# Down projection of a SwiGLU block: two passes over halves of the tokens instead of halves of the outputs

## The chip, the cores and the metric

The kernel runs on one core of a Trainium2 chip. The metric is the device time of one execution in microseconds (us): 2367.51 is the median of three runs of the kernel before.

## The reference, cut to what matters

One residual block: a token mixer, then a SwiGLU feed-forward, each followed by a layer norm over `ALPHA * x + gate * f(u)`. The change touches the very end only:

```python
x = layer_norm(ALPHA * x + g1 * h, ln1_g[l], ln1_b[l])
u = layer_norm(x) * (1.0 + sc2) + sh2
h = (silu(u @ w_gate) * (u @ w_up)) @ w_down      # (1024, 2816) @ (2816, 1024)
x = layer_norm(ALPHA * x + g2 * h, ln2_g[l], ln2_b[l])
```

All is float32. There are 1024 tokens and 1024 channels; `g2` is one row of 1024 channels, computed earlier and kept in DRAM (`g_d[1]`).

## The kernel before, in words

Precise products are made of two parts: every operand is split into a rounded value ("hi") and the rest ("lo"), and `Dense.mm` (L79) issues three matmuls per product: lo times hi (L81), hi times lo (L82), hi times hi (L83), each 128x512. `Dense.load` (L67) brings a 128x1024 block into `raw`, casts it to hi on ACT (L75) and subtracts to get lo on DVE (L76); `split` (L190) does the same for a tile at hand (L191, L192).

The gate and up projections write h, transposed, to DRAM as 22 blocks `h_d[k]` of 128 hidden features by 1024 tokens (stores at L1264, in `group`). The down projection then runs in two passes over **halves of the output channels**, `nh` = 0 and 1 (L1314 on). In each pass the eight PSUM banks `pss` hold eight token tiles `tt` of 128 tokens by 512 channels. Step k loads `h_d[k]` (512 KB) and half of the weights of block k (256 KB, `load_wd`, L1284), multiplies the weights by the gate row `g2r` on POOL (L1287), splits both, and issues 24 matmuls: 8 tiles of 3. The first 20 steps (pass 0) or 16 steps (pass 1) run step by step; the last 2 or 6 are kept as a "tail" and run tile by tile, so that the tiles end one after the other.

`finish` (L1293) ends a tile of a pass: it loads half of the residual x1 (L1295), computes `ALPHA * x1 + ps` straight from PSUM into `acc` (L1297) and takes statistics (L1298). Only in pass 1, when both channel halves of a token are known, `normalise_out` (L1302) scales and stores: all 8 token tiles, both halves each, behind the last six steps.

The order of the instructions on each engine is a scheduler's: it may move an instruction ahead of others within an engine's queue, in a fixed order that is then run as it stands. Waits come from buffers: `raw`, `wh`, `wl` exist twice, `st` (narrow raw blocks) and `sg` (used for x1) twice, `cw` (narrow hi and lo) three times.

Of the kernel before, what the change touches and what calls it, by code (L numbers as in the profile page):

```python
# [9 lines left out]
F32 = mybir.dt.float32  # L10
F32R = mybir.dt.float32r
# [21 lines left out]
P = 128  # L33
# [88 lines left out]
def hybrid_block(ctx, tc, x, w_mod, w_ada, w_blk, w_i, w_ba, w_bb, w_o, w_g, w_u, w_d,  # L122
# [871 lines left out]
    with tc.tile_pool(name="big2", bufs=4, reuse_waits="tile") as big2:  # L994
# [202 lines left out]
        with tc.tile_pool(name="fp", bufs=2, reuse_waits="tile") as fp, \  # L1197
# [23 lines left out]
            def group(gi):  # L1221
# [34 lines left out]
                for j, c in ((3, c22), (1, c12), (2, c21)):  # L1256
                    if up:
                        V.tensor_tensor(sg[:, j, :], sg[:, j, :], c, op=ALU.mult)
                    else:
                        act(c, c, AF.Silu)  # L1260
                if up:
# [5 lines left out]

            for gi in range(NFT):
                group(gi)


            halves = (slice(0, TH), slice(TH, D))
            stats = fp.tile([P, TT, 2, 6], F32, name="stats", bufs=1)
            NL_ = 6
# [4 lines left out]
            acc = [bigp.tile([P, TT, TH], F32, tag="big", name=f"acc{nh}") for nh in range(2)]  # L1279

            def load_h(k, into=None):
                return dn.load(h_d[k], None, into)

            def load_wd(k, nh, into=None):  # L1284
                raw = fp.tile([P, TH], F32, tag="st", name="wdr")
                nc.sync.dma_start(out=raw, in_=w_d[k, nh])
                G.tensor_tensor(raw, raw, g2r[:, halves[nh]], op=ALU.mult)  # L1287
                c = fp.tile([P, 2, TH], F32R, tag="cw", name="wd", bufs=3) if into is None else into
                S.copy(c[:, 0, :], raw)
                V.tensor_tensor(c[:, 1, :], raw, c[:, 0, :].bitcast(F32), op=ALU.subtract)  # L1290
                return c[:, 0, :], c[:, 1, :]

            def finish(nh, tt, ps):  # L1293
                x1 = fp.tile([P, 4, TH], F32, tag="sg", name="x1f")[:, 0, :]
                nc.sync.dma_start(out=x1, in_=x1_d[tt][:, halves[nh]])  # L1295
                a_ = acc[nh][:, tt, :]
                V.scalar_tensor_tensor(a_, x1, ALPHA, ps, op0=ALU.mult, op1=ALU.add)  # L1297
                V.bn_stats(stats[:, tt, nh, :], a_)  # L1298
                if nh:
                    normalise_out(tt, norm_scalars(stats[:, tt, :, :], fp))  # L1300

            def normalise_out(tt, mv):  # L1302
                for nh in range(2):
                    a_, sl = acc[nh][:, tt, :], halves[nh]
                    if nh and tt < TT - 1:
                        S.activation(a_, a_, AF.Identity, bias=mv[:, 3:4], scale=mv[:, 2:3])
                        V.tensor_tensor(a_, a_, lg2[:, sl], op=ALU.mult)
                        G.tensor_tensor(a_, a_, lb2[:, sl], op=ALU.add)
                    else:
                        V.scalar_tensor_tensor(a_, a_, mv[:, 0:1], lg2[:, sl], op0=ALU.subtract, op1=ALU.mult)  # L1310
                        V.scalar_tensor_tensor(a_, a_, mv[:, 2:3], lb2[:, sl], op0=ALU.mult, op1=ALU.add)
                    nc.sync.dma_start(out=out[tt][:, sl], in_=a_)

            for nh in range(2):  # L1314
# [104 lines left out]
```

## Time and profile before

| | us |
|---|---|
| median of 3 runs (lowest, highest) | 2367.51 (2366.99, 2368.29) |
| the profiled execution's own time | 2364.6 |
| its span, first to last instruction | 2362.8 |
| PE busy (x12412 matmuls) | 2248.6, 95% of the span |
| DVE busy | 1599.0, 68% |
| ACT busy | 1043.6, 44% |
| POOL busy | 391.4, 17% |

The profiled execution lies 2.9 us under the median. A PE that is busy 95% of the time says little of where a stage loses time; for that the stretches and the timeline of single engines are needed. The down projection begins at about 2098.8 us of the span.

### The profile page before, as it was taken

The page shows a single profiled execution, that of the slowest core. Times are in us where ns is not written, and L with a number is a line of the kernel's source. Part 1 is how long each engine was busy: PE and PEld are TensorE (multiplying, and loading weights), DVE is VectorE, ACT ScalarE, POOL GpSimd, SP SyncE. Part 2 cuts the span into 40 slices and gives each one's busy share as a digit, 9 for nine tenths or more (in the row PEclk, how much of TensorE's full clock was granted, in tenths as well). Part 3 has the DMA queues.
Part 4 walks back from the last instruction along what each step waited for, and adds up shares of the span by engine and source line. Part 5 has one row for each costly group of instructions (what it writes and reads, how often), then busy time and mean ns, then how long its engine had stood idle before and what let it go on. Part 6 is the DMA issues. An engine that isn't in the chain of part 4 may idle for free.

```text
span 2362.8 us, 32206 instructions
## 1 busy us (share of the span) xinstructions
PE 2248.6 (95%) x12412; PEld 1825.3 (77%) x12412; DVE 1599.0 (68%) x2548; ACT 1043.6 (44%) x1839; POOL 391.4 (17%) x239
## 2 busy tenths in 40 slices
PE   7899999999999999998997999999899999999996
PEld 4678888977777787776775888888788888888785
DVE  5966656538887658898976533458977666655547
ACT  3533333137666646777775421223633323322232
POOL 0600010012221221222222000004400000023234
PEclk9999999999999999999998999999999999999999
DMA  7334325601111232344454743432232222244544
GB/s 276 103 138 145 129 81 184 225 32 50 59 55 55 79 106 64 125 132 119 151 156 148 259 149 122 137 127 107 68 133 99 85 75 96 81 152 145 163 152 155
DMA packets 116033, 290.23 MB, mean 123 GB/s; under 512 B 12324, under 2 KB 27172, under 8 KB 115880
## 3 DMA queue, kind: packets, MB, share of 16 engines
q1 hardware_dynamic: 115880, 288.19, 36.7%
q8 instruction: 97, 1.59, 0.3%
q14 instruction: 56, 0.46, 0.1%
HBM read 234.52 MB, written 53.62 MB: 122 GB/s over the span
## 4 chain that ended last, share of the span: by engine, by line
PE 68%; DVE 14%; ACT 6%; DMA 4%; POOL 2%; issue 1%; SPq 0%; POOLq 0%; DVEq 0%; ACTq 0%
PE dps L81 8%; PE dps L83 8%; PE dps L82 8%; PE fps L81 8%; PE fps L82 8%; PE fps L83 8%; PE dqs L81 4%; PE dqs L83 4%; PE dqs L82 4%; DVE eb L657 1%; PE hps L83 1%; PE hps L81 1%; PE hps L82 1%; DVE xTm L813 1%; DVE e L649 1%
## 5 line engine op out<-in xcount | busy, mean ns | idle before, releaser
L81 PE MATMUL dps<-uh,wl 128*128 128x512 f32 x800 | 332.0, 415 | 2.5 <-DVE ge L405 2.5
L83 PE MATMUL dps<-uh,wh 128*128 128x512 f32 x800 | 318.4, 398 | 0.0
L82 PE MATMUL dps<-ul,wh 128*128 128x512 f32 x800 | 317.1, 396 | 0.0
L75 ACT CAST wh<-raw 128x1024 fp32r<-128x1024 f32 x113 | 118.6, 1050 | 261.6 <-PE fps L83 147.0
L76 POOL TENSOR_TENSOR wl<-raw,wh 128x1024 fp32r<-128x1024 f32 x50 | 129.6, 2592 | 548.5 <-ACT wh L75 528.3
L81 PEld LDWEIGHTS dps<-uh,wl 128*128 128x128 f32 x800 | 155.6, 195 | 36.9 <-issue 9.7
L83 PEld LDWEIGHTS dps<-uh,wh 128*128 128x128 f32 x800 | 152.7, 191 | 33.6
L82 PEld LDWEIGHTS dps<-ul,wh 128*128 128x128 f32 x800 | 153.5, 192 | 28.4 <-issue 0.9
L1287 POOL TENSOR_TENSOR wdr<-wdr,rws 128x512 f32<-128x512 f32 x44 | 71.3, 1624 | 528.8 <-DVE sg L1216 369.0
L82 PE MATMUL dqs<-yp,wh 128*128 128x512 f32 x384 | 149.3, 390 | 0.0
L83 PE MATMUL dqs<-yp,wh 128*128 128x512 f32 x384 | 149.1, 389 | 0.0
L81 PE MATMUL dqs<-yp,wl 128*128 128x512 f32 x384 | 148.3, 390 | 0.4 <-ACT yp L191 0.4
L76 DVE TENSOR_TENSOR wl<-raw,wh 128x1024 fp32r<-128x1024 f32 x63 | 79.5, 1261 | 98.0 <-ACT wh L75 98.0
L191 ACT CAST cw<-raw 128x512 fp32r<-128x512 f32 x131 | 80.8, 622 | 129.2 <-PE fps L83 88.8
L81 PE MATMUL fps<-t,cw 128*128 128x512 f32 x352 | 137.0, 389 | 0.7 <-ACT p L1177 0.7
L82 PE MATMUL fps<-t,cw 128*128 128x512 f32 x352 | 136.9, 389 | 0.0
L83 PE MATMUL fps<-t,cw 128*128 128x512 f32 x352 | 136.9, 389 | 0.0
L81 PE MATMUL fps<-wd,wl 128*128 128x512 f32 x304 | 119.1, 392 | 2.8 <-DVE wl L76 2.8
L82 PE MATMUL fps<-wd,wh 128*128 128x512 f32 x304 | 118.8, 391 | 0.0
L83 PE MATMUL fps<-wd,wh 128*128 128x512 f32 x304 | 118.6, 391 | 0.0
L192 DVE TENSOR_TENSOR cw<-raw,cw 128x512 fp32r<-128x512 f32 x109 | 79.8, 734 | 40.7 <-ACT cw L191 39.4
L179 POOL TENSOR_TENSOR mv<-mv,kc 128x1 f32<-128x1 f32 x32 | 28.5, 898 | 419.2 <-DVE mv L178 410.7
(368 smaller groups left out, 5654.2 us busy)
## 6 DMA issues: line engine op xcount, KB each, us to landing
raw<-in_w_blk_dram SPq DMA_DIRECT2D x78, 512.0 KB, 3.3
raw<-h_d SPq DMA_DIRECT2D x44, 512.0 KB, 3.5
wa<-in_w_ada_dram SPq DMA_DIRECT2D x32, 512.0 KB, 4.4
ac<-ac_d SPq DMA_DIRECT2D x32, 512.0 KB, 4.8
raw<-in_w_g_dram SPq DMA_DIRECT2D x26, 512.0 KB, 3.8
raw<-in_w_u_dram SPq DMA_DIRECT2D x26, 512.0 KB, 3.5
wdr<-in_w_d_dram SPq DMA_DIRECT2D x44, 256.0 KB, 3.2
h_d<-sg SPq DMA_DIRECT2D x18, 512.0 KB, 2.9
```

The lines of the kernel that those rows point to most:

```text
L75: nc.scalar.copy(wh, raw)
L76: (eng or self.lo).tensor_tensor(wl, raw, wh.bitcast(F32), op=ALU.subtract)
L81: nc.tensor.matmul(ps, sl, mh, start=first, stop=False)
L82: nc.tensor.matmul(ps, sh, ml, start=False, stop=False)
L83: nc.tensor.matmul(ps, sh, mh, start=False, stop=last)
L179: G.tensor_tensor(mv[:, 2:3], mv[:, 1:2], kc[:, 2:3], op=ALU.pow)
L191: S.copy(hi, src)
L192: eng.tensor_tensor(lo, src, hi.bitcast(F32), op=ALU.subtract)
L649: V.tensor_tensor(d.rearrange("p (n h j) -> p n h j", h=2, j=c), view(e, t0, (2 * c, n), (T + c, 2), (1, c)), view(r, t0 // 4 + c // 4 - 1 ...
L657: V.tensor_tensor(d.rearrange("p h (n j) -> p h n j", j=8), view(e, t0, (T, 2), (8, TH // 8), (1, 8)), view(r, t0 // 4, (T // 4, 2), (2, T ...
L813: V.scalar_tensor_tensor(d[:, o:], ps[:, o + j - 3:TH + j - 3], cw(j), d[:, o:], op0=ALU.mult, op1=ALU.add)
L1287: G.tensor_tensor(raw, raw, g2r[:, halves[nh]], op=ALU.mult)
```

## The change

The passes go over **halves of the tokens**, `p` = 0 and 1, instead of halves of the channels. The eight banks hold 4 token tiles by 2 channel halves. Step k loads half of `h_d[k]` (256 KB) and the whole weight block (512 KB, `fetch_hw`). Weights are no longer multiplied by `g2r` on POOL; `evict` multiplies by it on DVE when a bank is read. The residual is added in a second DVE instruction (`residual`), 512 or 1024 wide. After pass 0 four token tiles are complete over all channels, and `complete` normalises and stores them during the steps of pass 1; the other four end behind the last six steps. The scaling at the end is two DVE instructions per tile, 1024 wide, but for the last tile; the instruction on ACT (L1306), the one on POOL (L1308) and the small one at L181 are gone. The first fetch is emitted ahead of the last h stores (`ahead`).

```diff
-            def load_wd(k, nh, into=None):
-                raw = fp.tile([P, TH], F32, tag="st", name="wdr")
-                nc.sync.dma_start(out=raw, in_=w_d[k, nh])
-                G.tensor_tensor(raw, raw, g2r[:, halves[nh]], op=ALU.mult)
-                c = fp.tile([P, 2, TH], F32R, tag="cw", name="wd", bufs=3) if into is None else into
-                S.copy(c[:, 0, :], raw)
-                V.tensor_tensor(c[:, 1, :], raw, c[:, 0, :].bitcast(F32), op=ALU.subtract)
+            def fetch_hw(p, k):
+                rw = wp.tile([P, D], F32, tag="raw", name="wdr")
+                nc.sync.dma_start(out=rw.rearrange("p (h n) -> p h n", h=2), in_=w_d[k].rearrange("h p n -> p h n"))
+                rh = fp.tile([P, TH], F32, tag="st", name="hr")
+                nc.sync.dma_start(out=rh, in_=h_d[k][:, HF[p]])
+                return rh, rw
...
+            def step(ps, ops, tt, nh, first, last):
+                c, wd = ops
+                ts_ = slice(P * (tt % 4), P * (tt % 4) + P)
+                ns_ = slice(TH * nh, TH * nh + TH)
+                dn.mm(ps, c[:, 0, ts_], c[:, 1, ts_], wd[0][:, ns_], wd[1][:, ns_], first, last)
...
+                group(gi, (lambda: held.append(fetch_hw(0, 0))) if gi == NFT - 1 else None)
...
-                V.scalar_tensor_tensor(a_, x1, ALPHA, ps, op0=ALU.mult, op1=ALU.add)
+            def evict(tt, nh, ps):
+                sl = slice(TH * nh, TH * nh + TH)
+                V.tensor_tensor(acc[tt // 4][:, tt % 4, sl], ps, g2r[:, sl], op=ALU.mult)
+
+            def residual(tt, x1, sl):
+                a_ = acc[tt // 4][:, tt % 4, :]
+                V.scalar_tensor_tensor(a_[:, sl], x1[:, sl], ALPHA, a_[:, sl], op0=ALU.mult, op1=ALU.add)
...
+            def normalise_out(tt, sls):
+                a_ = acc[tt // 4][:, tt % 4, :]
+                mv = norm_scalars(stats[:, tt, :, :], fp, False)
+                for sl in sls:
+                    V.scalar_tensor_tensor(a_[:, sl], a_[:, sl], mv[:, 0:1], lg2[:, sl], op0=ALU.subtract, op1=ALU.mult)
+                    V.scalar_tensor_tensor(a_[:, sl], a_[:, sl], mv[:, 2:3], lb2[:, sl], op0=ALU.mult, op1=ALU.add)
+                    nc.sync.dma_start(out=out[tt][:, sl], in_=a_[:, sl])
...
+            for p in range(2):
+                tts = range(4 * p, 4 * p + 4)
+                pss = {(tt, nh): bank() for tt in tts for nh in range(2)}
+                nk = NFT - (NL if p else 2)
+                for k in range(nk):
+                    ops = parts(*(held.pop() if held else fetch_hw(p, k)))
+                    for tt in tts:
+                        for nh in range(2):
+                            step(pss[tt, nh], ops, tt, nh, k == 0, False)
+                    if ready and k % 2:
+                        complete(ready.pop(0))
...
+                tail = [parts(*fetch_hw(p, k), into[q]) for q, k in enumerate(range(nk, NFT))]
+                for tt in tts:
+                    if p:
+                        x1 = load_x1(tt)
+                    for nh in range(2):
+                        for q, ops in enumerate(tail):
+                            step(pss[tt, nh], ops, tt, nh, False, q == len(tail) - 1)
+                        evict(tt, nh, pss[tt, nh])
+                        if p:
+                            residual(tt, x1, halves[nh])
+                    if p:
+                        normalise_out(tt, halves if tt == TT - 1 else whole)
```

What it does to the scheduler's order, at three places. First **DVE at the switch from pass 0 to pass 1** (`wl_18040` is the lo of the h block that opens pass 1; `acc0`, `stats` belong to tiles of pass 0). Before:

```order
L1290 TENSOR_TENSOR wd_18046<-wdr_18043,wd_18046 128x512
L1297 SCALAR_TENSOR_TENSOR acc0_17195<-x1f_17955,fps_17197 128x512
L1297 SCALAR_TENSOR_TENSOR acc0_17195<-x1f_17965,fps_17198 128x512
L1298 BN_STATS stats_17190<-acc0_17195 128x6 x2
L1297 SCALAR_TENSOR_TENSOR acc0_17195<-x1f_17975,fps_17199 128x512
L1298 BN_STATS stats_17190<-acc0_17195 128x6
L1297 SCALAR_TENSOR_TENSOR acc0_17195<-x1f_17985,fps_17200 128x512
L1298 BN_STATS stats_17190<-acc0_17195 128x6
L1297 SCALAR_TENSOR_TENSOR acc0_17195<-x1f_17995,fps_17201 128x512
L76 TENSOR_TENSOR wl_18040<-raw_18037,wh_18039 128x1024
```

With the change (`wl_17996` is now the lo of the weight block, `fps_17208` the last bank of pass 0):

```order
L1307 TENSOR_TENSOR acc0_17199<-fps_17206,rws_17195 128x512
L177 BN_AGGR mv_18066<-stats_17194 128x2
L1311 SCALAR_TENSOR_TENSOR acc0_17199<-x1f_18143,acc0_17199 128x1024
L1307 TENSOR_TENSOR acc0_17199<-fps_17207,rws_17195 128x512
L1307 TENSOR_TENSOR acc0_17199<-fps_17208,rws_17195 128x512
L192 TENSOR_TENSOR wl_17996<-wdr_17991,wh_17995 128x1024
L192 TENSOR_TENSOR hp_18032<-hr_18028,hp_18032 128x512
L192 TENSOR_TENSOR wl_18031<-wdr_18026,wh_18030 128x1024
L178 TENSOR_TENSOR mv_18066<-mv_18066,kc_78 128x1
L1325 SCALAR_TENSOR_TENSOR acc0_17199<-acc0_17199,mv_18066,rws_17195 128x1024
```

All eight banks are now emptied ahead of the split that opens pass 1, and only two of the residual instructions stand ahead of it.

Second, **PE at the same place**. Before, the last matmul of pass 0 and the first of pass 1:

```order
L83 MATMUL fps_17204<-wd_17946,wh_17939 128x512
L81 MATMUL fps_18029<-wd_18046,wl_18040 128x512
L82 MATMUL fps_18029<-wd_18046,wh_18039 128x512
L83 MATMUL fps_18029<-wd_18046,wh_18039 128x512
L81 MATMUL fps_18030<-wd_18046,wl_18040 128x512
```

With the change (`wh` is the cast of the weight block, `hp` both parts of the h half):

```order
L83 MATMUL fps_17208<-wh_17920,hp_17922 128x512
L81 MATMUL fps_17983<-wh_17995,hp_17997 128x512
L81 MATMUL fps_17984<-wh_17995,hp_17997 128x512
L81 MATMUL fps_17985<-wh_17995,hp_17997 128x512
L81 MATMUL fps_17986<-wh_17995,hp_17997 128x512
L81 MATMUL fps_17987<-wh_17995,hp_17997 128x512
L81 MATMUL fps_17988<-wh_17995,hp_17997 128x512
L81 MATMUL fps_17989<-wh_17995,hp_17997 128x512
L81 MATMUL fps_17990<-wh_17995,hp_17997 128x512
L82 MATMUL fps_17983<-wl_17996,hp_17997 128x512
```

The first matmul of pass 1 read the wide lo before; now eight matmuls that do not read it stand ahead of the first that does.

Third, **DVE at the end**, the last tile. Before (`fps_18036` is the last bank):

```order
L1297 SCALAR_TENSOR_TENSOR acc1_17196<-x1f_18928,fps_18036 128x512
L1307 TENSOR_TENSOR acc1_17196<-acc1_17196,rws_17191 128x512
L1298 BN_STATS stats_17190<-acc1_17196 128x6
L177 BN_AGGR mv_18932<-stats_17190 128x2
L178 TENSOR_TENSOR mv_18932<-mv_18932,kc_78 128x1
L1310 SCALAR_TENSOR_TENSOR acc0_17195<-acc0_17195,mv_18932,rws_17191 128x512
L181 SCALAR_TENSOR_TENSOR mv_18932<-mv_18932 128x1
L1310 SCALAR_TENSOR_TENSOR acc1_17196<-acc1_17196,mv_18932,rws_17191 128x512
L1311 SCALAR_TENSOR_TENSOR acc0_17195<-acc0_17195,mv_18932,rws_17191 128x512
L1311 SCALAR_TENSOR_TENSOR acc1_17196<-acc1_17196,mv_18932,rws_17191 128x512
```

With the change (`fps_17990` is the last bank):

```order
L1307 TENSOR_TENSOR acc1_17200<-fps_17989,rws_17195 128x512
L1311 SCALAR_TENSOR_TENSOR acc1_17200<-x1f_18805,acc1_17200 128x512
L1314 BN_STATS stats_17194<-acc1_17200 128x6
L1307 TENSOR_TENSOR acc1_17200<-fps_17990,rws_17195 128x512
L1311 SCALAR_TENSOR_TENSOR acc1_17200<-x1f_18805,acc1_17200 128x512
L1314 BN_STATS stats_17194<-acc1_17200 128x6
L177 BN_AGGR mv_18849<-stats_17194 128x2
L178 TENSOR_TENSOR mv_18849<-mv_18849,kc_78 128x1
L1325 SCALAR_TENSOR_TENSOR acc1_17200<-acc1_17200,mv_18849,rws_17195 128x512 x2
L1326 SCALAR_TENSOR_TENSOR acc1_17200<-acc1_17200,mv_18849,rws_17195 128x512 x2
```

The last bank needs one DVE instruction more, and the first half of the last tile has its statistics before the last bank is ready.

## Rows read from the trace of the kernel before

**Rows 1.** The page's first line.
```profile
span 2362.8 us, 32206 instructions
```
**Rows 2.** Stretches: us, then busy us (instructions) by engine, granted TensorE clock, DMA share, GB/s.
```profile
2110.00:2160.00 50.00, 50.00 (x222) 41.44 (x221) 26.31 (x19) 15.21 (x20) 14.67 (x9) 1.00 0.47 148
2220.00:2280.00 60.00, 58.27 (x250) 48.15 (x251) 31.34 (x31) 17.14 (x23) 16.59 (x11) 0.97 0.51 165
2280.00:2330.00 50.00, 47.26 (x207) 38.29 (x206) 30.10 (x36) 17.16 (x21) 17.19 (x11) 1.00 0.48 153
2345.00:2363.00 18.00, 1.71 (x8) 1.09 (x6) 13.17 (x26) 1.69 (x3) 6.58 (x6) 0.68 0.39 138
```
**Rows 3.** PE in order of time at the switch: start, duration, [idle before <-releaser].
```profile
2218.51 0.39 PE L83 MATMUL fps<-wd,wh 128*128 128x512 f32 x1
2221.73 0.79 PE L81 MATMUL fps<-wd,wl 128*128 128x512 f32 x1 [2.83 <-DVE wl L76]
...
2225.20 0.39 PE L83 MATMUL fps<-wd,wh 128*128 128x512 f32 x1
```
**Rows 4.** DVE in order of time at the switch.
```profile
2216.52 0.69 DVE L1297 SCALAR_TENSOR_TENSOR acc<-x1f,fps 128x512 f32<-128x512 f32 x1 [2.27 <-DMA x1f<-x_d]
...
2219.85 0.69 DVE L1297 SCALAR_TENSOR_TENSOR acc<-x1f,fps 128x512 f32<-128x512 f32 x1 [0.60 <-DMA x1f<-x_d]
2220.45 1.22 DVE L76 TENSOR_TENSOR wl<-raw,wh 128x1024 fp32r<-128x1024 f32 x1
```
**Rows 5.** ACT in order of time, a step of pass 0 and the switch.
```profile
2207.85 1.06 ACT L75 CAST wh<-raw 128x1024 fp32r<-128x1024 f32 x1 [3.87 <-PE fps L83]
...
2218.26 1.99 ACT L75 CAST wh<-raw 128x1024 fp32r<-128x1024 f32 x2 [8.84 <-PE fps L83]
```
**Rows 6.** PE in order of time, the last six steps of pass 1.
```profile
2310.45 0.39 PE L81 MATMUL fps<-wdl,hl 128*128 128x512 f32 x1
...
2313.17 0.39 PE L81 MATMUL fps<-wdl,hl 128*128 128x512 f32 x1
2315.40 0.50 PE L81 MATMUL fps<-wdl,hl 128*128 128x512 f32 x1 [1.84 <-DVE hl L76]
...
2318.76 0.50 PE L82 MATMUL fps<-wdl,hl 128*128 128x512 f32 x1 [0.89 <-DVE wdl L1290]
```
**Rows 7.** DVE in order of time, fourth and sixth wide split of these six.
```profile
2314.12 1.23 DVE L76 TENSOR_TENSOR hl<-raw,hl 128x1024 fp32r<-128x1024 f32 x1 [0.96 <-ACT hl L75]
...
2320.01 1.23 DVE L76 TENSOR_TENSOR hl<-raw,hl 128x1024 fp32r<-128x1024 f32 x1 [0.48 <-ACT hl L75]
```
**Rows 8.** PE in order of time, the last matmul.
```profile
2346.32 0.39 PE L83 MATMUL fps<-wdl,hl 128*128 128x512 f32 x1
```
**Rows 9.** DVE in order of time, the end (the last row is two instructions).
```profile
2350.51 0.69 DVE L1298 BATCH_NORM_STATS2 stats<-acc 128x6 f32<-128x512 f32 x1
...
2355.00 0.69 DVE L1298 BATCH_NORM_STATS2 stats<-acc 128x6 f32<-128x512 f32 x1
...
2357.63 0.75 DVE L1310 SCALAR_TENSOR_TENSOR acc<-acc,mv,rws 128x512 f32<-128x512 f32 x1
2358.29 1.41 DVE L1311 SCALAR_TENSOR_TENSOR acc<-acc,mv,rws 128x512 f32<-128x512 f32 x2
```
**Rows 10.** Groups of instructions of the down projection: count, then busy us, mean ns.
```profile
L1287 POOL TENSOR_TENSOR wdr<-wdr,rws 128x512 f32<-128x512 f32 x44 | 71.3, 1624 | 528.8 <-DVE sg L1216 369.0 <-DMA wdr<-in_w_d_dram 155.6 <-DVE wl L76 4.3
...
L1290 DVE TENSOR_TENSOR wd<-wdr,wd 128x512 fp32r<-128x512 f32 x38 | 51.6, 1358 | 4.2 <-ACT wd L1289 4.2
```
**Rows 11.** One line of the program, a 1024-wide scaling elsewhere: duration ns min/median/max.
```profile
L1161 DVE SCALAR_TENSOR_TENSOR x<-xr,mv,lgr x8: 1272/1280/1281, 1594.5 to 1669.6; 128x1024 f32<-128x1024 f32 x8
```
**Rows 12.** The load queue in order of time: h of a step of pass 0 is issued.
```profile
2204.75 0.32 SPq L70 DMA_DIRECT2D raw<-h_d  x1
```
**Rows 13.** DMA issues: KB each, median us from issue to landing; down projection, then whole program.
```profile
raw<-h_d SPq DMA_DIRECT2D x41, 512.0 KB, 3.5
...
was<-in_w_mod_dram SPq DMA_DIRECT2D x16, 512.0 KB, 7.0
```

More of the change, by code (lines that the diff above doesn't have):

```diff
@@ L1219, in first_products, with group @@
                 return p1
-            def group(gi):
+            def group(gi, ahead=None):
                 i, up = divmod(gi, 2)
@@ L1260, in group @@
                         act(c, c, AF.Silu)
+                if ahead:
+                    ahead()
                 if up:
@@ new lines, in hybrid_block @@
+            acc = [bigp.tile([P, 4, D], F32, tag="big", name=f"acc{p}") for p in range(2)]
+            def evict(tt, nh, ps):
[4 more added lines that the diff above has]
+                V.scalar_tensor_tensor(a_[:, sl], x1[:, sl], ALPHA, a_[:, sl], op0=ALU.mult, op1=ALU.add)
+                for nh in range(2):
+                    if sl.start <= TH * nh < sl.stop:
+                        V.bn_stats(stats[:, tt, nh, :], a_[:, TH * nh:TH * nh + TH])
@@ new lines, in load_x1 @@
+            def load_x1(tt):
+                x1 = fp.tile([P, 4, TH], F32, tag="sg", name="x1f")[:, 0:2, :].rearrange("p a b -> p (a b)")
+                nc.sync.dma_start(out=x1, in_=x1_d[tt])
+                return x1
+            def normalise_out(tt, sls):
[5 more added lines that the diff above has]
+                    nc.sync.dma_start(out=out[tt][:, sl], in_=a_[:, sl])
@@ new lines, in hybrid_block, with complete @@
+            halves, whole = (slice(0, TH), slice(TH, D)), (slice(0, D),)
+            ready = []
+            def complete(tt):
+                x1 = load_x1(tt)
+                residual(tt, x1, whole[0])
+                normalise_out(tt, whole)
+            for p in range(2):
[9 more added lines that the diff above has]
+                        complete(ready.pop(0))
+                into = [None] * 2
+                if p:
+                    ht = [pool.tile([P, 4, 2, TH], F32R, tag=t, name="htl") for pool, t in ((bigp, "big"), (big2, "big2"))]
+                    wt = [big2.tile([P, 2, 2, D], F32R, tag="big2", name="wtl") for _ in range(3)]
+                    into = [(ht[q // 4][:, q % 4], (wt[q // 2][:, q % 2, 0, :], wt[q // 2][:, q % 2, 1, :])) for q in range(NL)]
+                tail = [parts(*fetch_hw(p, k), into[q]) for q, k in enumerate(range(nk, NFT))]
+                for tt in tts:
+                    if p:
+                        x1 = load_x1(tt)
+                    for nh in range(2):
[4 more added lines that the diff above has]
+                            residual(tt, x1, halves[nh])
+                    if p:
+                        normalise_out(tt, halves if tt == TT - 1 else whole)
+                    else:
+                        ready.append(tt)
```

58 lines of the change are left out of this document (9 added, 49 removed).

## The prediction

> **What bounds the kernel now.** I read the stretches first, then PE in order of time wherever a stretch is not full, then the engine that released it. In the plain steps PE is the bound: 50.00 of 50.00 us busy at clock 1.00 [rows 2]. The 13th matmul of the six-step tail starts 2.72 us after the first [rows 6], so one costs 2.72/12 = 0.227 us and a step of 24 costs 5.44. Nothing done to other engines there can show. The down projection loses time at three places.
>
> *The switch of the passes.* The last matmul of pass 0 starts at 2218.51, the next at 2221.73: 3.22 instead of 0.23, so 2.99 lost. From there the clock stays at its lower level, 1.2 GHz, for eight matmuls (0.97 over the stretch [rows 2]): 2225.20 - 2221.73 = 3.47 instead of 1.81, another 1.66. Together 4.65 [rows 3]. The releaser is DVE's wide split L76. DVE, which runs its queue in order, had stood twice for a residual load (2.27 and 0.60) in instructions ahead of that split [rows 4].
>
> *The tail of pass 1.* It has 8 x 18 = 144 matmuls, 32.65 us, from 2310.45 [rows 6]; the last one's slot ends at 2346.32 + 0.23 = 2346.55 [rows 8]. That is 36.10, so 3.45 lost, in waits of 1.84 and 0.89 for late operands and short ones around them [rows 6].
>
> *The end.* From 2346.55 to the span's end at 2362.8 [rows 1, 8] PE has nothing to do: 16.25 us. DVE is busy for 13.17 of the last 18 [rows 2]: eight tiles end 18 matmuls (4.08 us) apart, but DVE starts a tile's statistics only every 4.49 (2350.51, 2355.00 [rows 9]), and the backlog is worked off when PE is done. Statistics of the last tile start only at 2355.00, 8.45 after the last matmul [rows 9].
>
> **The change, part by part.**
>
> *Start.* The fetch ahead of the last stores: the load queue's order with the change has the first block's load in the same place as before, one tile's h stores ahead of the last ones, since the scheduler had moved it there already. PE had no gap at that boundary either. 0 us.
>
> *Plain steps.* The 24 matmuls and 768 KB stay. POOL's 44 multiplications (1.62 each) go; DVE's narrow split, 1.36 on the mean beside them [rows 10], should fall to the 0.69 of a 512-wide instruction alone [rows 4]. All of this is hidden under PE: 0. If the cover were gone it would be 0.67 x 38 = 25 us, but rows 2 show no gap. The wider weight load: h was issued at 2204.75 [rows 12], right when its buffer came free. The next cast, at 2207.85 [rows 5], is of the block before it, so its own is due one step later, 2213.3 in the steady rhythm. That leaves 8.5 us against a landing of 3.5 for 512 KB [rows 13]. Hidden.
>
> *Switch, -4.0.* With the change the first eight matmuls of pass 1 need only the cast of the weight block and a narrow h that DVE split long before. That cast starts when its buffer is released, three matmuls ahead of the end of pass 0, as in 2218.26 [rows 5], that is 0.48 before the last slot ends (2218.74), and takes 1.06: PE starts 0.65 after the end, and 8 x 0.227 = 1.8 later, at +2.45, it wants the wide lo. DVE must empty the eighth bank (0.69, from +0.2; it may be +1.0 when it is done, since a 1024-wide residual stands ahead) and split (1.22): +2.3. So 0.65 lost instead of 4.65. The residual loads of these tiles are issued while the gate and up projections run, so DVE does not stand for them. Bounds: 0 (DVE late by as much as before) and -4.65.
>
> *DVE in pass 1, 0.* New there: four tiles of residual, statistics, two 1024-wide scalings and a store, in the first six steps. The queue's order lets me add it up to the split that step 5 needs: 6 wide splits at 1.22, 9 wide scalings and residuals at 1.22 (1.28 long [rows 11], but the next starts before the end: two 512-wide ones take 1.41 and not 1.50 [rows 9]), 5 narrow splits and 6 statistics at 0.60 to 0.69, seven one-column ones taken at 0.17 each, 1.2: 7.3 + 11.0 + 6.6 to 7.6 + 1.2 = 26.1 to 27.1, from +1.0: done by +27.1 to +28.1. Step 5 starts at 0.65 + 5 x 5.44 = +27.85 and wants it one matmul later, +28.1. It just fits; earlier steps have 1.5 us and more. Bounds 0 and +5 (below: it can gain nothing).
>
> *Tail, -1.0.* The six late steps still go through two wide buffers: load, cast, split, free, load. I take their times over, since 512 KB and a wide split are in the chain as before: fourth cast done at 2314.1, its lo at 2315.35, the sixth lo at 2321.24 [rows 7], which against the tail's start of 2310.45 is +3.65, +4.9 and +10.8. The new PE order has 9 matmuls first (2.04), then one that needs the fourth cast: 1.6 lost; then 4 before the fourth lo: 0.35; about 0.45 for the sixth. 2.4 instead of 3.45. Bounds: +2 (a load of the chain one us later costs that twice) and -3.45.
>
> *End, -7.6.* Four tiles instead of eight end there, 8.16 us of matmuls apart, with about 6.5 us of DVE work each (6 narrow instructions 3.6 to 4.1, two wide 2.4, two one-column ones 0.35): no backlog. Behind the last matmul: read the bank times g2r, add the residual, 2 x 0.65; statistics to the last scaling as before, from 2355.00 to 2358.29 + 1.41 = 2359.70, 4.70, less 0.6 since the second L1310 no longer stands behind L181 and POOL's result [rows 9]; then the store, 2362.8 - 2359.70 = 3.1. 1.3 + 4.1 + 3.1 + 0.1 = 8.6 instead of 16.25. The extra DVE instruction per bank is paid only here, once. Bounds -6.5 and -8.5.
>
> **Sum:** -4.0 - 1.0 - 7.6 = -12.6, so the profiled execution (2364.6) would come to 2352.0; the runs' median lies 2.9 above it, and goes to **2354.9**. About 0.2%, 4.7 us, is what a measurement of this kernel can tell from no change.
>
> **Rivals.**
>
> *DVE overruns in pass 1.* The margin at step 5 is under 1 us by my sum. Anything that makes the queue slower, such as loads of x1, stores and operands sharing the DMA there, moves PE's wait to steps 3 to 6, and a wait of near 3 us brings the low clock, 1.66 more. 2 to 5 us: 2357 to 2360. For: the sum is tight. Against: the instructions' spacing is taken from rows. The Trainium skill (VectorE: DVE Perf Modes, The DRAIN you can't avoid) says that the next instruction does not start until the one before has left the pipe; by that full durations count, 26 wide and narrow ones some 0.07 longer each, 1.8 more, and PE would wait about 1.5: 2356.5. This case's trace disagrees so far: 1.41 for two of 0.75 [rows 9].
>
> *The clock falls at the shorter gaps.* It fell behind 2.83 idle, not behind 1.84 or 0.89 (1.00 in that stretch [rows 2, 6]). If one of the new gaps is caught it costs 1.66 [rows 3], two 3.3: 2356.6 to 2358.2. The Trainium skill (TensorE: Matmul & The Clock Gate, A second HAM failure mode) describes short idle times between groups of matmuls that let the clock swing; no gap of that size did so here.
>
> *The end stays long.* If the change does not take the backlog away, because scalings of earlier tiles still stand ahead of the last tile on DVE, only -5.0 is left: 2362.5, which counts as the same.
>
> *Slower: the weight loads become the bound.* The block's load now has 2 KB runs and sits in the chain of two buffers. The plain steps have 8.5 us for it; past that every us costs a us in each of some 36 steps. A landing of 9.0 would cost 18 and eat the whole gain: 2373. For: other 512 KB loads took 7.0 in a busier stretch of this program [rows 13]. Against: 3.5 here, at half the DMA's share.
>
> **How the numbers follow.** Forecast as summed, 0.62; DVE overrun 0.17; clock 0.10; end stays long 0.06; weight loads 0.05. Low end: all three terms at their best, -4.65 - 3.45 - 8.5 = -16.6, 2351. High end: DVE overrun at its worst, with a poor tail (+2): 2362; beyond it lie most of the last two, 1 in 10. Faster by over 0.2% (under 2362.8): the first three, 0.89, less 0.02 for several small misses at once, 0.87. Same: the long end, these 0.02 and 0.01 of the weight loads, 0.09. Slower: the rest of the weight loads, 0.04.
>
> **What would show it.** Right: at the switch a PE gap under 1 us and no stretch at low clock; PE full through steps 0 to 6 of pass 1; about 2.4 us of gaps in the tail; 8 to 9 us from the last matmul to the end; no busy POOL but for the small powers; narrow splits at 0.69. Wrong: PE waits for a wide lo in steps 2 to 6 of pass 1; waits for weight loads in plain steps; over 12 us behind the last matmul.

## The result, and the profile after

The changed kernel takes 2355.72 us in the median of six runs, the kernel before 2367.59 beside it: a ratio of 0.9945, 95% interval 0.9932 to 0.9958. It is faster; the prediction was 2354.9, range 2351 to 2362.

The profiled execution's span is 2353.3 us against 2362.8 [rows 1], 9.5 less. That is not the size of the change: the same work ahead of the down projection took 3.9 us more in this execution, whose down projection starts at 2102.73 and not at 2098.79. That start varies from one profile to the next whatever the layout: three kernels with the layout before begin at 2098.8, 2100.6 and 2105.4, those with the new one between 2099.3 and 2107.3. An effect of the change ahead of the down projection is not seen in them, though one of a us or two would be lost in this spread. So everything below is measured from the first matmul of the down projection to the end, the **stage**, which repeats to 0.01 us in the two profiles of the changed kernel (250.57 and 250.56); the kernel before has one profile. Stretches of the kernel before, cut at the first matmul, the switch, step 8 of pass 1, the tail, the last matmul (columns as in [rows 2]):

```profile
2098.79:2218.74 119.95, 119.95 (x529) 98.89 (x528) 64.11 (x54) 31.97 (x41) 33.65 (x21) 1.00 0.49 157
2218.74:2262.00 43.26, 40.44 (x172) 33.23 (x172) 24.47 (x25) 12.41 (x17) 11.13 (x7) 0.96 0.55 175
2262.00:2310.45 48.45, 48.45 (x216) 40.12 (x214) 24.51 (x21) 16.60 (x21) 16.47 (x10) 1.00 0.49 159
2310.45:2346.55 36.10, 33.36 (x145) 26.61 (x143) 28.23 (x48) 9.00 (x11) 15.47 (x13) 1.00 0.45 146
2346.55:2362.80 16.25, 0.16 (x1) 0.00 (x0) 11.62 (x24) 1.63 (x2) 6.20 (x6) 0.65 0.36 140
```

The same five of the changed kernel:

```profile
2102.73:2222.63 119.90, 119.90 (x529) 98.76 (x527) 47.65 (x57) 31.96 (x41) 0.00 (x0) 1.00 0.48 158
2222.63:2266.00 43.37, 42.91 (x190) 35.40 (x190) 32.76 (x43) 13.56 (x18) 6.70 (x4) 1.00 0.69 233
2266.00:2310.42 44.42, 44.42 (x198) 36.78 (x197) 17.90 (x20) 16.14 (x21) 0.00 (x0) 1.00 0.51 171
2310.42:2344.97 34.55, 33.59 (x145) 26.53 (x143) 26.78 (x39) 3.67 (x4) 4.37 (x3) 1.00 0.34 119
2344.97:2353.30 8.33, 0.16 (x1) 0.00 (x0) 5.10 (x9) 0.00 (x0) 0.92 (x1) 0.70 0.17 63
```

Read the first number (the length) and the second (PE busy). Pass 0 is full in both. Switch and steps of pass 1 together go from 91.71 to 87.79, the tail from 36.10 to 34.55, the end from 16.25 to 8.33: -3.92, -1.55, -7.92, in all -13.4. In the first stretch POOL went from 33.65 us to nothing and DVE from 64.11 to 47.65, and PE did not notice.

PE in order of time at the switch, which answers to [rows 3]:

```profile
2222.40 0.39 PE L83 MATMUL fps<-wh,hp 128*128 128x512 f32 x1
2223.24 2.11 PE L81 MATMUL fps<-wh,hp 128*128 128x512 f32 x8 [0.46 <-ACT wh L191]
2225.19 0.39 PE L82 MATMUL fps<-wl,hp 128*128 128x512 f32 x1
```

The gap is 0.61 (0.84 less one slot, the 0.23 from one matmul's start to the next), the eight covering matmuls take 1.95 instead of 1.81, and the granted clock stays at 1.00: 0.75 lost instead of 4.65. The releaser is the cast, not DVE. DVE in order of time, last eviction, split (compare [rows 4]), and step 5's wide split 25 us on:

```profile
2222.82 0.69 DVE L1307 TENSOR_TENSOR acc<-fps,rws 128x512 f32<-128x512 f32 x1 [0.15 <-PE fps L83]
2223.43 1.22 DVE L192 TENSOR_TENSOR wl<-wdr,wh 128x1024 fp32r<-128x1024 f32 x1
...
2247.80 1.22 DVE L192 TENSOR_TENSOR wl<-wdr,wh 128x1024 fp32r<-128x1024 f32 x1
...
2251.86 1.23 DVE L192 TENSOR_TENSOR wl<-wdr,wh 128x1024 fp32r<-128x1024 f32 x1 [1.04 <-ACT wh L191]
```

The split that step 5 needs is done at 2249.02, 26.4 behind the end of pass 0 (2222.63), where 28.1 was the limit; for step 6 DVE waits for the cast again, so its backlog is gone. The tail's largest gap, which answers to [rows 6], and the end of DVE, which answers to [rows 9]:

```profile
2315.47 0.73 PE L81 MATMUL fps<-wtl,htl 128*128 128x512 f32 x2 [0.91 <-ACT wtl L191]
```

```profile
2345.17 0.69 DVE L1307 TENSOR_TENSOR acc<-fps,rws 128x512 f32<-128x512 f32 x1 [0.60 <-PE fps L83]
2345.89 0.69 DVE L1311 SCALAR_TENSOR_TENSOR acc<-x1f,acc 128x512 f32<-128x512 f32 x1
2346.62 0.69 DVE L1314 BATCH_NORM_STATS2 stats<-acc 128x6 f32<-128x512 f32 x1
2347.35 0.21 DVE L177 BATCH_NORM_AGGREGATE mv<-stats 128x2 f32<-128x12 f32 x1
2347.59 0.16 DVE L178 TENSOR_TENSOR mv<-mv,kc 128x1 f32<-128x1 f32 x1
2347.67 1.41 DVE L1325 SCALAR_TENSOR_TENSOR acc<-acc,mv,rws 128x512 f32<-128x512 f32 x2
2348.99 1.41 DVE L1326 SCALAR_TENSOR_TENSOR acc<-acc,mv,rws 128x512 f32<-128x512 f32 x2
```

DVE is idle and waiting for PE when the last bank comes: the backlog is gone, and what is left of the end is one chain, 5.2 us of DVE and 2.9 of the store behind it.

### The profile page after: what moved, and what is told of

Read it like the earlier page. It is cut to its first block, busy times and chain, and to the rows that moved or that the text cites. A ratio compares the mean times of both kernels' runs of the same rounds, so it can differ in the third digit from the quotient of the medians.

```text
span 2353.3 us, 32121 instructions
## 1 busy us (share of the span) xinstructions
PE 2251.6 (96%) x12412; PEld 1827.9 (78%) x12412; DVE 1573.2 (67%) x2545; ACT 1036.3 (44%) x1832; POOL 314.7 (13%) x188
## 4 chain that ended last, share of the span: by engine, by line
PE 73%; DVE 10%; ACT 6%; DMA 3%; POOL 1%; issue 1%; SPq 0%; DVEq 0%; POOLq 0%; ACTq 0%
PE dps L81 9%; PE dps L82 9%; PE dps L83 9%; PE fps L81 9%; PE fps L82 9%; PE fps L83 8%; PE dqs L82 4%; PE dqs L83 4%; PE dqs L81 4%; DVE eb L657 1%; PE hps L83 1%; PE hps L82 1%; PE hps L81 1%; PE yi L897 1%; DVE e L649 1%
## 5 line engine op out<-in xcount | busy, mean ns | idle before, releaser
L75 ACT CAST wh<-raw 128x1024 fp32r<-128x1024 f32 x75 | 78.4, 1046 | 112.3 <-PE dqs L83 103.5
L82 PE MATMUL fps<-wl,hp 128*128 128x512 f32 x304 | 118.4, 389 | 0.0
L83 PE MATMUL fps<-wh,hp 128*128 128x512 f32 x304 | 118.3, 389 | 0.0
L81 PE MATMUL fps<-wh,hp 128*128 128x512 f32 x304 | 117.0, 390 | 0.5 <-ACT wh L191 0.5
L192 DVE TENSOR_TENSOR wl<-wdr,wh 128x1024 fp32r<-128x1024 f32 x38 | 46.5, 1224 | 105.0 <-ACT wh L191 105.0
L191 ACT CAST wh<-wdr 128x1024 fp32r<-128x1024 f32 x38 | 40.1, 1054 | 147.3 <-PE fps L83 146.1
```

The lines of the kernel that those rows point to most:

```text
L75: nc.scalar.copy(wh, raw)
L81: nc.tensor.matmul(ps, sl, mh, start=first, stop=False)
L82: nc.tensor.matmul(ps, sh, ml, start=False, stop=False)
L83: nc.tensor.matmul(ps, sh, mh, start=False, stop=last)
L191: S.copy(hi, src)
L192: eng.tensor_tensor(lo, src, hi.bitcast(F32), op=ALU.subtract)
```

## The experiments

Eleven kernels ran, the changed kernel among them. The stage and its parts in us (pass 0; switch with the 16 steps of pass 1; tail; end), and the ratio of the whole time to the kernel before with its interval:

| kernel | pass 0 | to the tail | tail | end | stage | ratio |
|---|---|---|---|---|---|---|
| before | 119.95 | 91.71 | 36.10 | 16.25 | 264.0 | 1 |
| changed | 119.90 | 87.79 | 34.55 | 8.33 | 250.6 | 0.9945 (0.9932, 0.9958) |
| gate_late | 119.91 | 97.47 | 33.99 | 20.21 | 271.6 | 1.0035 (1.0023, 1.0046) |
| gate_load | 124.15 | 97.35 | 42.97 | 8.64 | 273.1 | 1.0050 (1.0034, 1.0066) |
| all_at_end | 119.89 | 87.83 | 34.81 | 19.27 | 261.8 | 0.9994 (0.9981, 1.0007) |
| lo_first | 119.88 | 90.87 | 34.46 | 8.32 | 253.5 | 0.9960 (0.9944, 0.9977) |
| x1_late | 119.93 | 91.03 | 36.28 | 16.51 | 263.8 | 0.9985 (0.9970, 0.9999) |
| dve_plus1 | 119.89 | 87.83 | 34.58 | 8.34 | 250.6 | 0.9949 (0.9938, 0.9961) |
| pool_beside | 119.89 | 101.62 | 35.29 | 8.39 | 265.2 | 0.9987 (0.9973, 1.0001) |
| load_twice | 124.97 | 92.55 | 39.10 | 8.57 | 265.2 | 0.9987 (0.9972, 1.0002) |
| tail_early | 119.89 | 87.79 | 32.64 | 8.34 | 248.7 | 0.9948 (0.9935, 0.9961) |
| tail_switch | 119.87 | 86.85 | 32.64 | 8.41 | 247.8 | 0.9936 (0.9923, 0.9949) |

The ratios resolve about 3 us; the stages tell the rest.

**gate_late: the gate's move alone.**

```diff
-                G.tensor_tensor(raw, raw, g2r[:, halves[nh]], op=ALU.mult)
...
-                V.scalar_tensor_tensor(a_, x1, ALPHA, ps, op0=ALU.mult, op1=ALU.add)
+                V.tensor_tensor(a_, ps, g2r[:, halves[nh]], op=ALU.mult)
+                V.scalar_tensor_tensor(a_, x1, ALPHA, a_, op0=ALU.mult, op1=ALU.add)
```

> The kernel before (channel halves), with one part of the change alone: weights are no longer multiplied by the gate row on POOL; each bank is multiplied by it on DVE when it is read, and the residual is a second DVE instruction. Theory (the gain is in the token halves, the gate's move by itself frees engines that were hidden): plain steps stay full and gain 0; at the switch three DVE pairs more stand ahead of the wide split, so the gap of 2.99 grows to 5 to 7 us; at the end each of eight tiles needs 0.65 more on a DVE that is behind already (4.49 per tile against 4.08), so 16.25 grows to about 21. In all +7 to +9 us on the kernel before. Rival (POOL and the slow narrow splits did cost time before): plain steps or tail get shorter, -1 to -3 us in all.

Stage +7.6. DVE at the switch, in order of time; the last bank was complete at 2225.33:

```profile
2228.71 1.27 DVE L1296 TENSOR_TENSOR acc<-fps,rws 128x512 f32<-128x512 f32 x2
2229.91 1.43 DVE L1297 SCALAR_TENSOR_TENSOR acc<-x1f,acc 128x512 f32<-128x512 f32 x2
2231.26 1.28 DVE L1298 BATCH_NORM_STATS2 stats<-acc 128x6 f32<-128x512 f32 x2
2232.45 2.35 DVE L76 TENSOR_TENSOR wl<-raw,wh 128x1024 fp32r<-128x1024 f32 x2
```

PE waits 8.22 us for that split, and the wait here is DVE's own work, with no load in it: a little beyond the 5 to 7 expected. The end grew by 3.96. The rival holds in one place: without POOL in the chain the tail became 2.1 shorter. It is outweighed.

**gate_load: the token halves alone.** The weights are scaled on POOL as before, and banks are read by a copy.

```diff
+                G.tensor_tensor(rw, rw, g2r, op=ALU.mult)
                 split(*wd, rw, V)
...
-                V.tensor_tensor(acc[tt // 4][:, tt % 4, sl], ps, g2r[:, sl], op=ALU.mult)
+                V.tensor_copy(acc[tt // 4][:, tt % 4, sl], ps)
```

> The changed kernel (token halves), with the gate back on POOL, 1024 wide at the weight load; banks are read by a plain DVE copy, all else as changed. Theory (DVE in the first six steps of pass 1 has 1.7 us to spare, and DVE instructions beside POOL are longer: 1.36 on the mean for a narrow split against 0.69 alone): about 16 us of POOL in five steps, 0.41 us of DVE lost per us of POOL, 6.7 us in all, so PE waits 3 to 5 us in steps 3 to 6 of pass 1, with 1.66 more if the clock falls; in the tail 3.2 us of POOL stands in the chain of each late block, and its stalls grow from 1.9 to 5 to 9 us; the end stays at 8.3. In all +6 to +13 us on the changed kernel, about the time of the kernel before. Rival (the layout alone makes the gain, POOL's work stays hidden as it was): 0 to +2 us.

Stage +22.5 on the changed kernel: the right sign, much too small. Each half of the change by itself is slower than the kernel before, together they are 13.4 faster. One reservation: with token halves every weight block is loaded twice in full, so POOL has 44 multiplications 1024 wide here (2.40 us in the median) and had 44 of 512 [rows 10] before; this half of the change brings POOL more work than it had. Of the 22.5, 9.6 are in pass 1, 8.4 in the tail and 4.3 in pass 0, where PE waits 2.31 for a wide lo in the first step and runs at a granted clock of 0.73 behind it from 2109.68 to 2116.00. One place in pass 1, POOL and then DVE:

```profile
2237.78 2.39 POOL L1285 TENSOR_TENSOR wdr<-wdr,rws 128x1024 f32<-128x1024 f32 x1
```

```profile
2237.79 3.46 DVE L1327 SCALAR_TENSOR_TENSOR acc<-acc,mv,rws 128x1024 f32<-128x1024 f32 x1 [0.45 <-POOL mv L179]
...
2241.78 2.31 DVE L192 TENSOR_TENSOR hp<-hr,hp 128x512 fp32r<-128x512 f32 x1
```

A 1.28 us instruction that begins with POOL's takes 3.46. I had put the loss at 0.41 us of DVE per us of POOL, from means of the kernel before; at a collision it is the whole rest of POOL's instruction. Whether the loss came from this or from POOL standing in the chain of each block was open, and the next run tells.

**pool_beside: POOL's work, out of the chain.** Nothing reads its result.

```diff
+                if k < (20, 16)[p]:
+                    G.tensor_tensor(acc[1][:, k % 4, :], rw, g2r, op=ALU.mult)
                 return rh, rw
...
-                group(gi, (lambda: held.append(fetch_hw(0, 0))) if gi == NFT - 1 else None)
+                group(gi)
```

(The second edit takes out `ahead`: the fetch now uses `acc` and `g2r`, which the program makes only behind that loop.)

> The changed kernel, with a 1024-wide multiplication on POOL in each plain step of both passes that reads the weight block just loaded and writes a buffer that nothing reads: POOL's work of the run with the gate at the load, but in nobody's chain. Theory (POOL and DVE keep each other out: DVE instructions beside POOL took 2.0 to 3.5 us instead of 0.69 to 1.28 there): steps 3 to 6 of pass 1 lose 5 to 8 us in waits for the wide lo, with the clock at times, as there (7.3 in three gaps); the tail, which has no such POOL work, stays near 1.9, the end at 8.3: stage 256 to 260. Rival (the loss there was the 2.4 us of POOL in the chain from load to cast): 0 to 1 us, stage 250.6 to 251.6.

Stage +14.6, all but 0.8 of it between the switch and the tail (101.62 against 87.79); pass 0, where DVE has time to spare, loses nothing. The 13.8 are beyond the 5 to 8 expected: 2.8 more are lost at the switch and 8.9 in waits of four of the steps behind it, and the clock falls once (0.73 from 2265.68 to 2272.00). DVE stands for no cast and no load in these steps, so a load buffer that POOL holds longer is not the cause. So the collision alone costs more in pass 1 than gate_load lost there. In gate_load's tail the chain shows too: four casts in a row wait 5.55, 2.47, 3.53 and 4.34 us for POOL. POOL, DVE and PE at one step:

```profile
2245.72 2.72 POOL L1280 TENSOR_TENSOR acc<-wdr,rws 128x1024 f32<-128x1024 f32 x1 [5.39 <-DMA wdr<-in_w_d_dram]
```

```profile
2246.13 3.39 DVE L192 TENSOR_TENSOR wl<-wdr,wh 128x1024 fp32r<-128x1024 f32 x1
```

```profile
2249.58 0.50 PE L82 MATMUL fps<-wl,hp 128*128 128x512 f32 x1 [2.38 <-DVE wl L192]
```

The split began 0.41 behind POOL's instruction and ended at 2249.52, 1.08 behind its end at 2248.44: about its own 1.22 later, as if it had not run beside it at all. The Trainium skill (SBUF — State Buffer, Who interferes with whom) says that a DVE instruction with two SBUF inputs contends with a GpSimd instruction that reads SBUF, that what they contend for is an exclusive lock, and that the order of issue decides who blocks. The trace agrees.

**all_at_end: tiles of pass 0 completed late.**

```diff
-                    if ready and k % 2:
-                        complete(ready.pop(0))
...
+                        complete(ready.pop(0))
                         normalise_out(tt, halves if tt == TT - 1 else whole)
```

> The changed kernel, but the tiles of pass 0 are completed between the tiles of pass 1 behind the last six steps, not during the steps of pass 1. Theory (the end fell from 16.25 to 8.3 because four tiles' work left it): the first tile is still done at the switch, three more bring 3 x 5.4 = 16 us of DVE work into a stretch with about 1.7 us free per tile, so 9 to 12 us come back behind the last matmul: end 17 to 20, whole time +9 to +12. Rival (the end is shorter because the chain of the last tile is shorter, the backlog would have been small): end 8 to 10, +0 to +2.

Stage +11.2, end 19.27, little else moved: 10.9 of the end's time is work of pass 0's tiles that the steps of pass 1 otherwise hide. The rival falls. The end of this run (columns as in [rows 2]; DVE is the third busy time):

```profile
2347.63:2366.90 19.27, 0.16 (x1) 0.00 (x0) 16.26 (x27) 0.00 (x0) 4.91 (x4) 0.56 0.34 133
```

DVE works 16.26 us behind the last matmul, against 5.10 in the changed kernel. The end is also 3.0 longer than that of the kernel before (16.25), so apart from the early tiles nothing in the change, as this run orders it, shortens the end.

**lo_first: the eight covering matmuls undone.** In step 0 of pass 1 the wide lo is read first.

```diff
+                if first and tt >= 4:
+                    PE.matmul(ps, c[:, 0, ts_], wd[1][:, ns_], start=True, stop=False)
+                    PE.matmul(ps, c[:, 1, ts_], wd[0][:, ns_], start=False, stop=False)
+                    PE.matmul(ps, c[:, 0, ts_], wd[0][:, ns_], start=False, stop=False)
+                    return
```

> The changed kernel, but in the first step of pass 1 each bank's first matmul reads the lo of the weight block, so that nothing of pass 1 can start ahead of the wide split. Theory (eight matmuls that need only the cast cover DVE's eviction and split): PE starts when the split is done, 2.0 us behind the last slot of pass 0 instead of 0.6: about +1.4, and if the clock falls behind that idle time 1.66 more, +3.0. The trace shows which: the durations and spacing of the eight matmuls behind the gap. Rival (what shortened the gap was only that no x1 load stands in DVE's queue): the gap stays under 1 us, +0.

Stage +3.0: a gap of 2.08, and then the low clock. PE in order of time, then the stretch of this step:

```profile
2226.12 0.39 PE L83 MATMUL fps<-wh,hp 128*128 128x512 f32 x1
2228.43 0.50 PE L1293 MATMUL fps<-wl,hp 128*128 128x512 f32 x1 [1.92 <-DVE wl L192]
2228.76 0.39 PE L1294 MATMUL fps<-wh,hp 128*128 128x512 f32 x1
2228.99 0.40 PE L1295 MATMUL fps<-wh,hp 128*128 128x512 f32 x1
2229.23 0.45 PE L1293 MATMUL fps<-wl,hp 128*128 128x512 f32 x1
2229.48 0.63 PE L1294 MATMUL fps<-wh,hp 128*128 128x512 f32 x1
```

```profile
2228.43:2235.62 7.19, 7.19 (x25) 5.76 (x25) 7.06 (x9) 0.48 (x1) 1.52 (x1) 0.76 0.86 292
```

The step takes 7.19 instead of 5.44 at a granted clock of 0.76; the matmuls of 0.63 are those at 1.2 GHz. So of the 3.1 lost up to the tail, 1.5 is the longer gap and 1.6 the lower clock behind it.

**x1_late: the residual waits undone, in the kernel before.**

```diff
-                V.scalar_tensor_tensor(a_, x1, ALPHA, ps, op0=ALU.mult, op1=ALU.add)
-                V.bn_stats(stats[:, tt, nh, :], a_)
+                if nh:
+                    residual(nh, tt, ps)
+                else:
+                    V.tensor_copy(a_, ps)
...
+                    if nh and 4 <= k < 12:
+                        residual(0, k - 4, acc[0][:, k - 4, :])
```

(`residual` holds the load, the addition and the statistics that stood in `finish`.)

> The kernel before, where pass 0 reads its banks by a plain DVE copy and adds the residual later, in the steps of pass 1, so that no eviction waits for a residual load. Theory (the gap of 2.99 at the switch of the kernel before is 0.9 us of waits for residual loads and 2.1 of eviction and wide split that nothing covers): the gap goes to 1.9 to 2.1, and the clock falls or not: with it the switch loses 3.6 to 3.8, without it about 2.0, against 4.65: stage 261.3 to 263.2 against 264.0; end as before, 16.2. Rival (residual loads were the whole of the gap): the switch loses under 1 us, stage about 260.

The gap went from 2.99 to 2.39 and the clock fell all the same, so the stretch to the tail lost 0.7 less (91.03 against 91.71); tail and end came out 0.4 longer, so the stage gained only 0.26, less than expected. By this run residual loads were 0.7 us of the kernel before's switch.

```profile
2221.01 0.68 DVE L1298 COPY acc<-fps 128x512 f32<-128x512 f32 x1
2221.61 2.34 DVE L76 TENSOR_TENSOR wl<-raw,wh 128x1024 fp32r<-128x1024 f32 x2
```

Eviction and wide split follow each other without a wait here, and PE stands for both. The eviction still starts 0.53 behind the end of pass 0 (2220.48), since an addition of an earlier tile stands ahead of it on DVE.

**dve_plus1: more work for DVE in pass 1.**

```diff
                 residual(tt, x1, whole[0])
+                V.scalar_tensor_tensor(x1, x1, ALPHA, lb2, op0=ALU.mult, op1=ALU.add)
```

> The changed kernel with one 1024-wide DVE instruction more in the completion of each of the four tiles of pass 0 (it overwrites a buffer that nobody reads any more). Theory (DVE had 1.7 us to spare at step 5 of pass 1: its wide split was done 26.4 behind the end of pass 0 and needed at 28.1): four instructions at 1.13 to 1.22 are 4.5 to 4.9 us, so PE waits 2.8 to 3.2 us in all for a wide lo in steps 3 to 6, and 1.66 more if the clock falls behind it: stage 253.4 to 255.5 against 250.6. If every instruction had to be paid with its full duration and the spare time were smaller, up to +5. Rival (DVE's queue has hidden slack, since it also waits for casts and loads there): no wait, +0 to +1.

No wait at all, stage +0.07. My theory fell. DVE in order of time around step 5:

```profile
2248.22 1.22 DVE L192 TENSOR_TENSOR wl<-wdr,wh 128x1024 fp32r<-128x1024 f32 x1
...
2252.35 1.21 DVE L1335 SCALAR_TENSOR_TENSOR x1f<-x1f,rws 128x1024 f32<-128x1024 f32 x1
2253.47 1.22 DVE L192 TENSOR_TENSOR wl<-wdr,wh 128x1024 fp32r<-128x1024 f32 x1
```

Step 5's split was done 25.7 behind the end of pass 0, earlier than in the changed kernel. The order had been made anew: the fourth tile's statistics and scalings and its extra instruction now stand behind that split, ahead of those of steps 6 and 7. The 1.7 us at step 5 were where the order had put them, not what DVE has in reserve.

**load_twice: a costlier weight load.**

```diff
                 nc.sync.dma_start(out=rw.rearrange("p (h n) -> p h n", h=2), in_=w_d[k].rearrange("h p n -> p h n"))
+                if k < (20, 16)[p]:
+                    nc.sync.dma_start(out=rw.rearrange("p (h n) -> p h n", h=2), in_=w_d[k].rearrange("h p n -> p h n"))
```

> The changed kernel, with the load of the weight block issued twice in each plain step, the second over the first, so that a block costs the queue about twice as much and lands about twice as late (7 to 8 us instead of 3.9). Theory (the plain steps have some 8.5 us for it): plain steps of pass 0 stay full; in the first steps of pass 1, where residual loads and stores share the DMA, 0 to 3 us may be lost: stage 250.6 to 254. Rival (the load is near the bound already, the case in which the change would have made the kernel slower): past 8.5 us every us costs a us in each of 36 steps; at 9.5 that is 36 us, stage 270 to 300.

Stage +14.6, 5.1 in pass 0, 4.8 in pass 1 and 4.6 in the tail, and not as expected. The second load waits on the queue until the first has landed, the queue's own waits from 2105 to 2215 being

```profile
SPq L1278 <- DMA wdr<-in_w_d_dram: 64.0, 18, 4.3
```

(total, times, longest). From the first issue to the cast it was 8.2 to 10 us, not 7 to 8. So a block that takes that long does cost, 5.1 / 20 = 0.25 us a step, but the run mixes landing with a queue that stands still; it prices neither alone. In the changed kernel itself the spare time can be read: a load is issued at 2132.47 and its block cast at 2141.01, 8.54 later, while such loads land in 4.0 in the median (2110 to 2200).

**after_again, tail_early, tail_switch: can what is left be had?** after_again is the changed kernel as it stands.

> The changed kernel once more, on the chip of the runs beside it, as their measure: stage 250.6 from the first matmul of the down projection to the end; 0.75 us lost at the switch, 1.9 in the tail, 8.3 behind the last matmul. What the program does ahead of the down projection may differ by some us from one execution to the next, as it did between the two profiles (2098.8 and 2102.7 for the same instructions).

It came to 2357.73 us on this chip (the kernel before: 2369.62) and repeated the stage, the switch and the end. tail_early fetches four of the six late blocks inside pass 1:

```diff
...
+                    if p and k in (8, 10, 12, 14):
+                        tail.append(parts(*fetch_hw(p, nk + len(tail)), into[len(tail)]))
...
```

> The changed kernel, with four of the six late blocks fetched, cast and split between steps 8 to 15 of pass 1, one in every second step, into the buffers they already had; the last two behind them. Theory (the tail loses 1.9 us because its blocks pass through two load buffers one after the other and come late): every operand is there when the tail begins, its gaps go: stage -1.5 to -1.9, no new gap in the steps, whole time -1.5 to -1.9. Rival (three blocks in two steps are too many for the two load buffers): PE waits for a cast or a wide lo in steps 9 to 15, +1 to +5.

The tail is full, and no new gap appeared: stage -1.9.

```profile
2314.62:2347.26 32.64, 32.64 (x145) 26.85 (x143) 22.82 (x33) 0.00 (x0) 4.38 (x3) 1.00 0.21 81
```

The whole time did not show it (2358.21 against 2357.73): 1.9 us is less than the runs resolve, and the profiled execution began the stage 4.1 us later than after_again's (2106.94 against 2102.84).

tail_switch also lets the last two blocks of pass 0 use the late blocks' buffers:

```diff
...
+                into, tail = (spare if p else spare[4:]), []
...
-                into = [None] * 2
...
```

(`spare` are the six late buffers, made ahead of pass 0.)

> As the early tail, and the two blocks that end pass 0 also go to the late blocks' buffers, so that the two step buffers are free and the first two blocks of pass 1 are cast and split before pass 0 ends. Theory (the 0.75 us at the switch are the wait for a step buffer and the cast behind it): no gap at the switch, stage -2.3 to -2.6 against the changed kernel. Rival (in the load queue the block of step 2 now stands behind four residual loads and a store that waits for DVE): the gap moves to step 2 or 3, 1 to 3 us, and the gain is eaten: -1.5 to +1.

Its stretches:

```profile
2107.33:2227.20 119.87, 119.87 (x530) 99.32 (x529) 51.53 (x63) 34.70 (x44) 0.07 (x1) 1.00 0.52 171
2227.20:2314.05 86.85, 86.85 (x385) 71.91 (x383) 52.75 (x62) 31.22 (x39) 6.02 (x4) 1.00 0.60 203
2314.05:2346.69 32.64, 32.64 (x145) 26.85 (x143) 22.82 (x33) 0.00 (x0) 4.38 (x3) 1.00 0.22 81
2346.69:2355.10 8.41, 0.16 (x1) 0.00 (x0) 5.09 (x9) 0.00 (x0) 0.92 (x1) 0.67 0.17 62
```

PE is busy in every microsecond from its first matmul of the down projection to its last: stage -2.8, a little more than expected, and the fastest of all kernels here, 2355.16 against 2357.73 on the same chip. The two ratios' intervals overlap, so in the whole time that step is not shown, only in the stage. The gap did not move to step 2.

## Why the prediction was right

*Start and plain steps, 0.* Right: pass 0 is 119.90 against 119.95, POOL idle, narrow splits at 0.69. pool_beside runs without `ahead`: its load queue issues in the same order around that place, and its pass 0 takes 119.89; `ahead` was not taken out by itself. gate_late takes the same work off POOL and gains nothing in pass 0.

*Switch, -4.0.* Measured -3.9 (0.75 lost, 0.65 forecast). The wait itself was 0.61; the forecast's rows give 1.06 - 0.48 = 0.58, and 0.65 with a remainder that it does not name. The other 0.14 is the eight matmuls, 1.95 instead of 1.81. One reading was off without harm: of the two residual loads that stand ahead of the split, one is issued at 2108.59, 5.9 us into pass 0 and not before it; DVE waits for neither. The weights inside the term were not said: of the way back from 0.75 to 4.65, 3.1 is the order of the matmuls (lo_first), and x1_late puts the residual waits, which the prediction named as the cause of the late split, at 0.7. About half of the 3.1 is the lower clock.

*DVE in pass 1, 0.* Right: no wait. The sum was 27.1 to 28.1 and the measurement 26.4, though the margin read from it was not a real limit (dve_plus1). Two things in the sum were off and partly cancel: DVE waits 0.76 in all for POOL's small powers, which the sum left out, and its instructions take 24.8 and not 26.1 to 27.1. The rival of a DVE that overruns did not occur, but pool_beside shows it is real where something slows DVE that the order does not reckon with: 13.8 us between the switch and the tail. By full durations the sum would have been 1.8 more, but instructions that do not depend on each other follow sooner: a 1.22 split is followed 1.13 later (2223.43, then 2224.56), a 0.69 one 0.60 later. The Trainium skill (VectorE: DVE Perf Modes, The DRAIN you can't avoid) gives the rule of the emptied pipe, by which the prediction counted full durations, and adds that a next instruction that is not held starts earlier. The trace agrees with the addition.

*Tail, -1.0.* Measured -1.55: 1.9 lost instead of 2.4. tail_early shows that all of it was late blocks. The total came out better than its parts, and that is luck in part: the forecast put 1.6 of the 2.4 ahead of the fourth cast and nothing ahead of the fifth. ACT's casts of the fourth and the fifth weight block:

```profile
2311.47 1.05 ACT L191 CAST wtl<-wdr 128x1024 fp32r<-128x1024 f32 x1 [1.59 <-DMA wdr<-in_w_d_dram]
2314.37 1.04 ACT L191 CAST wtl<-wdr 128x1024 fp32r<-128x1024 f32 x1 [1.85 <-DMA wdr<-in_w_d_dram]
```

The fourth is done 2.10 behind the tail's start and not 3.65, and costs 0.1; the fifth is done 5.0 behind it, and PE's largest gap, 1.07 at 2315.47, waits for it.

*End, -7.6.* Measured -7.9: 8.33 instead of 8.6. all_at_end shows that the mechanism is the one named, work of four tiles moved under PE. What the shorter chain of the last tile is worth was not run by itself.

*The rivals.* The clock did not fall at the new gaps (0.61 at the switch, 0.91 idle in the tail; 1.00 in both stretches). The end did not stay long. Weight loads were not the bound; that limit was not priced by itself.

*The sum* was -12.6 against -13.4 in the stage. The median fell by 11.9, and the interval of the ratio is 9.9 to 16.1 us, so the two agree as far as the runs tell. One thing was not foreseen: executions differ by 4 us and more ahead of the stage, as much as a term of the sum. That the forecast of 2354.9 came within 1 us of the median is therefore partly luck: the same kernel had 2357.73 on another chip.

## What to carry to other kernels

Look for work that only one layout lets you finish early, and let it end under the bound engine; but count both halves of such a change together, since here each alone made the kernel slower (the token halves with twice the POOL work). Where a stage restarts, order the bound engine's instructions so that the first of them need the operand that is ready first: eight matmuls covered an eviction and a split, worth 3 us here, about half of it by the clock. When a few us matter in some 2360, compare the stage, cut at the same instructions, and not the whole time.

## What was not expected of the hardware

DVE and POOL did not share: beside a POOL instruction of 2.4 to 2.7 us, DVE instructions of 1.22 to 1.28 took 3.39 to 3.46, while a copy out of PSUM (gate_load, 2228.35) and statistics (2228.94), with one input each, took their 0.67 and 0.68 in the middle of POOL's 2226.34 to 2229.49. DVE instructions that depend on the one before follow at 0.72 to 0.73 (the end above), others of the same size at 0.60. The clock fell behind 1.92 us of idle time in lo_first, but not at once: four matmuls ran at full speed, then eight at 1.2 GHz; behind 1.84 in the kernel before's tail [rows 6] it did not fall. That is no limit, though. It did not fall behind 1.91 in gate_load (2245.28) nor behind 2.38 in pool_beside (2249.58, shown above), while it fell behind 2.24 in x1_late. In these runs the length of one gap alone does not say whether the clock falls. The stretch behind the 2.38, with the granted clock third from the end:

```profile
2249.58:2255.00 5.42, 5.42 (x24) 4.42 (x24) 5.04 (x6) 0.00 (x0) 2.04 (x2) 1.00 0.73 224
```
